# Convolution taps and gate tanh in two token halves, and a backward scan of one link per step, in a one-core hybrid encoder layer

## The chip, the cores and the metric

The kernel runs on one core of one Trainium2 chip, as one program. The metric is the device time of one execution in microseconds (us); of several runs the median counts. Five engines have queues of their own, each worked off in order: PE (TensorE, the matrix products), DVE (VectorE), ACT (ScalarE), POOL (GpSimd) and SP (SyncE, which here only issues transfers). PEld in the profile is the loading of weights into PE.

## The reference

One encoder layer for 1024 tokens of width 1024, all in float32. What the change touches is the state-space branch (SSD) and what goes ahead of it:

```python
def depthwise_conv_centred(u, w, bias):                 # 5 taps, padding 2 on both sides, per channel
    ...
    return out + bias.astype(u.dtype)

def ssd_branch(z, xbc, dt_raw, ...):
    xbc = jax.nn.silu(depthwise_conv_centred(xbc, conv_w, conv_b))
    xs, Bm, Cm = ...                                    # 32 heads of 64, 8 groups of B and C (state 128)
    dt = jax.nn.softplus(dt_raw + dt_bias)              # one for each direction
    y_fwd = ssd_chunked(xs, dt[:, :, 0], A[0], Bm, Cm)
    y_bwd = fl(ssd_chunked(fl(xs), fl(dt[:, :, 1]), A[1], fl(Bm), fl(Cm)))
    y = (y_fwd + y_bwd + d_skip * xs) * silu(z)
    ...                                                 # RMSNorm in 8 groups
```

`ssd_chunked` works in chunks of 128 tokens: within a chunk a masked product of C, B and the decays, and between chunks a scan `carry = carry * decay + state`, forward in one direction and backward in the other. The rest of the layer (windowed attention with a sink, gates `sigmoid(gate) * branch`, output projection, cross-attention into a normalised memory of 256 tokens, a squared-ReLU MLP, the final norm) is not touched.

## The kernel before

A matrix product in float32 is made of three passes with split operands (`mm3`, lines 85, 89 and 90): 8 such triples for 512 tokens by 128 channels, so 48 matmuls for all 1024 tokens. `phase0` normalises memory and input, writes the memory's keys and values, and computes the time steps (`dt_part`). `ssd_phase` then works through 8 groups of four heads. For each group it runs jobs on PE, in an order written out by hand: four convolution jobs (two tiles of x, one of B, one of C, numbers 0 to 3), one gate job, and one job for z. A convolution job computes a tile of 128 channels by 1024 tokens (`fm_chunks`, tokens 0 to 511 first: its "first half") into a PSUM tile `cps` of two banks; `conv_post` then makes ACT write weight 2 times the tile plus the bias into `acc`, DVE add the four other taps one after the other, ACT take a tanh and DVE multiply (SiLU). Such PSUM tiles have two buffers.

Between the triples of a job, at the counts in the table `at`, work on the scan of the group before is issued: `step(q, c)` for chunk c from 7 down to 0. On PE a step is `cb` of the next chunk (C times B), four small products with the decays `ef`, and `yo` (C times the carried states `prev`); on DVE it is the mask product of `ef` and `cb`, `t`, and three steps on `y`; on POOL two steps on `p1` and two affine selects on the decay rows, which ACT turns into `ef` and `eb` with eight exponentials. All jobs of a group but z's have a step, or the transposes of x (`tm_x`, in job 3), behind triple 8, that is between their halves, and most have another behind triple 16.

PE's order is that of the code (manual schedule). The order on the other engines is chosen by a scheduler when the program is built, and each engine then works through its own list. The backward chain of a group, six links of two POOL instructions each, is issued in `back` at the end of the z job. In `phase0` the row of norm weights for x is spread over 128 partitions by two matmuls (line 228) that stand behind the transposes of the normalised memory.

Of the kernel before, what the change touches and what calls it, by code (L numbers as in the profile page):

```python
# [7 lines left out]
F32 = mybir.dt.float32  # L8
F32R = mybir.dt.float32r
I32 = mybir.dt.int32  # L10
AF = mybir.ActivationFunctionType
ALU = mybir.AluOpType
# [4 lines left out]
P = 128  # L17
S = 1024
D = 1024
NT = 8  # L20
# [4 lines left out]
NEG = -1.0e30  # L25
# [139 lines left out]
def phase0(kx, ins, dr):  # L165
    nc, tc = kx.nc, kx.tc
    V, A, PE = nc.vector, nc.scalar, nc.tensor
    with tc.tile_pool(name="p0", bufs=1, side="right") as p0, tc.manual_schedule(engines={mybir.EngineType.PE}):
# [52 lines left out]
        wk.append(weight(ins["wxk"][1]))  # L221
        xs.append(load(ins["x"][P:2 * P]))
        gb = [psum_g(kx, "gb") for _ in range(2)]
        for h in range(2):
            PE.matmul(gb[0][:, h * 512:(h + 1) * 512], ones, gr[:, 0, h * 512:(h + 1) * 512], start=True, stop=True)
        for j in range(2):
            mem_split(rows(xm[j], gb[0]), j * P)
            PE.matmul(gb[1][:, j * 512:(j + 1) * 512], ones, gr[:, 1, j * 512:(j + 1) * 512], start=True, stop=True)
        kx.hT = [act_tiles(kx) for _ in range(2)]
        wv = []  # L230
        for t in range(NT):
# [15 lines left out]
def dt_part(kx, ins, dr, p0):  # L247
# [79 lines left out]
    for src, dst in ((keep, kx.coef), (acc, kx.ebias), (e, kx.ecs)):  # L327
# [3 lines left out]
            if j == 0:  # L331
                kx.tc.keep_in_program_order(t)
        A.activation(dst, pt.rearrange("p (j d s h) -> p s j d h", j=4, d=2, s=2), AF.Copy)
    conv_post(kx, kx.first, 2, cps)


def gate_block(kx, ins, dr, m, pool=None, pin=False):
# [22 lines left out]
def fm_chunks(kx, ps, w, halves=(0, 1)):  # L360
    ws = wsplit(w)
    for h in halves:
        for k in range(NK):
            mm3(kx, ps[:, h * 512:(h + 1) * 512], ws[k], act_pair(kx.hT[h], k), k == 0, k == NK - 1)
            yield
# [6 lines left out]
def conv_post(kx, q, i, ps):  # L372
    V, A = kx.nc.vector, kx.nc.scalar
    ca = kx.conv_pool
    tag = ("cx", "cx", "cB", "cC")[i]
    j = 4 * q.g + i
    cw = lambda k: kx.cw[:, 5 * j + k:5 * j + k + 1]
    acc = ca.tile([P, S], F32, tag=tag, bufs=2 if i < 2 else 1, name=tag)
    A.activation(acc, ps, AF.Identity, bias=kx.cb[:, j:j + 1], scale=cw(2))
    for k in (1, 3, 0, 4):  # L380
        o = k - 2
        if o < 0:
            V.scalar_tensor_tensor(acc[:, -o:], ps[:, :S + o], cw(k), acc[:, -o:], ALU.mult, ALU.add)
        else:
            V.scalar_tensor_tensor(acc[:, :S - o], ps[:, o:], cw(k), acc[:, :S - o], ALU.mult, ALU.add)  # L385
    th = ca.tile([P, S], F32, tag="tab", bufs=2, name="th")
    A.activation(th, acc, AF.Tanh)
    V.scalar_tensor_tensor(acc, th, 1.0, acc, ALU.add, ALU.mult)
    if i < 2:
        q.cx.append(acc)  # L390
    else:
        setattr(q, ("BT", "CT")[i - 2], acc)


def first_tiles(kx, ins, dr):

    q = kx.first = Group(0)
    ws = [wload(kx, ins["wssd"][0, i]) for i in range(2)]
    pss = [psum_g(kx, "cps") for _ in range(2)]
    for h in range(2):  # L400
        for i in range(2):
            for _ in fm_chunks(kx, pss[i], ws[i], (h,)):
                pass
    w = wload(kx, ins["wg"][0])
    gps = [kx.pp.tile([P, 512], F32, tag="p", name="gps") for _ in range(2)]
    for h in range(2):
        gemm_fm(kx, gps[h], w, kx.hT[h])
    for i in range(2):
        conv_post(kx, q, i, pss[i])
    gt = kx.conv_pool.tile([P, 2, 512], F32, tag="tab", bufs=2, name="gt")  # L410
    for h in range(2):
        kx.nc.scalar.activation(gt[:, h], gps[h], AF.Tanh, scale=0.5)
        kx.nc.sync.dma_start(dr.gt[0][h], gt[:, h])


def ssd_phase(kx, ins, dr):
# [4 lines left out]
    with tc.tile_pool(name="p1", bufs=1) as sp, tc.manual_schedule(engines={mybir.EngineType.PE}):  # L421
# [4 lines left out]
        def heads(ap):  # L426
            return ap.rearrange("p (h q) -> p h q", h=4)
# [3 lines left out]
        def conv_job(q, i):  # L431
            def load():
                return wload(kx, ins["wssd"][q.g, i])

            def run(w):
                ps = psum_g(kx, "cps")
                yield from fm_chunks(kx, ps, w)
                conv_post(kx, q, i, ps)
            return load, run

        def gate_job(m):
            def load():
                return wload(kx, ins["wg"][m])

            def run(w):
                ps = psum_g(kx, "gps")
                yield from fm_chunks(kx, ps, w)
                gt = ca.tile([P, 2, 512], F32, tag="tab", bufs=2, name="gt")
                for h in range(2):
                    A.activation(gt[:, h], ps[:, h * 512:(h + 1) * 512], AF.Tanh, scale=0.5)  # L450
                    nc.sync.dma_start(dr.gt[m][h], gt[:, h])
            return load, run
# [42 lines left out]
        def decay(q, d, c):  # L495
            o = 64 * d + 32 * (c // 4) + 4 * q.g
            return kx.dec[:, o:o + 4, c % 4:c % 4 + 1].broadcast_to([P, 4, 64])
# [15 lines left out]
            if c > 0:  # L513
                A.activation(prev[:, c - 1, 1], st[:, 256:], AF.Copy)

        def back(q):
            prev = q.prev
            for c in range(NT - 2, 0, -1):
                t = sp.tile([P, 256], F32, tag="p1", bufs=2, name="cb_t")
                G.tensor_tensor(heads(t), heads(prev[:, c, 1]), decay(q, 1, c), ALU.mult)  # L520
                G.tensor_tensor(prev[:, c - 1, 1], prev[:, c - 1, 1], t, ALU.add)  # L521

        def prep(q, c):
            b, j = c // 4, c % 4
            rows = sp.tile([P, 2, 4, P], F32, tag="rows", bufs=2, name="rows")
            for d in range(2):
                o = 64 * d + 32 * b + 4 * q.g
                nc.scalar.dma_start(rows[:, d], dr.cs[o:o + 4, j * P:(j + 1) * P].partition_broadcast(P))
            G.affine_select(out=rows[:, 0], in_=rows[:, 0], compare_op=ALU.is_ge, fill=NEG, base=0,  # L529
                            pattern=[[0, 4], [1, P]], channel_multiplier=-1)  # L530
            G.affine_select(out=rows[:, 1], in_=rows[:, 1], compare_op=ALU.is_ge, fill=NEG, base=0,  # L531
                            pattern=[[0, 4], [-1, P]], channel_multiplier=1)
            ef = q.efs[c] = sp.tile([P, 4, P], F32, tag="ef", bufs=3, name="ef")
            eb = sp.tile([P, 4, P], F32, tag="eb", bufs=2, name="eb")
            with tc.issue_after(q.zt[8 - c].ins) if c > 4 else ExitStack():
                for h in range(4):
                    o = 4 * q.g + h
                    A.activation(ef[:, h], rows[:, 0, h], AF.Exp, bias=kx.ebias[:, b, j, 0, o:o + 1])  # L538
                    A.activation(eb[:, h], rows[:, 1, h], AF.Exp, bias=kx.ebias[:, b, j, 1, o:o + 1])  # L539
            V.tensor_tensor(ef, ef, eb, ALU.add)  # L540
# [8 lines left out]
        def step(q, c):  # L549
# [23 lines left out]
            G.tensor_tensor(heads(p1), heads(q.xtok[:, c]), dsk[:, q.hs].unsqueeze(2).broadcast_to([P, 4, 64]), ALU.mult)  # L573
            if d1 - d0 == 2:
                G.tensor_tensor(p1, p1, t[:, 1], ALU.add)
            y = q.yz[j] = sp.tile([P, 256], F32, tag="yz", bufs=8, name="yz")
            V.tensor_tensor(y, cb[:, 256:], t[:, d0], ALU.add)
            V.tensor_tensor(y, y, p1, ALU.add)
# [23 lines left out]
        for g in range(NG):  # L602
# [10 lines left out]
            at = {8 * c + 8: [(state, q, c)] for c in range(NT)}  # L613
            at[4] = [(tm_b, q)]
            at[56] += [(prep, q, 7)]
            at[64] += [(prep, q, 6), (back, q), (mask, q, 7)]
            job(z_job(q), at)
        q = gs[7]
        job(gate_job(8), {6: [(step, q, 7)], 12: [(step, q, 6)]})
# [1092 lines left out]
```

## Time and profile before

| What | us |
|---|---|
| Median of 3 runs (2375.48 to 2376.95) | 2375.82 |
| Profiled execution, its own time | 2374.8 |
| Its span, first to last instruction | 2373.0 |
| PE busy | 2328.3 |
| DVE busy | 1567.7 |
| ACT busy | 1124.2 |
| POOL busy | 865.4 |

The profiled execution lies 1.0 us under the median and 1.8 us over its own span. A row of the timeline reads: start, duration, engine, line, operation, output from inputs, shape, count, and in brackets how long the engine had been idle and what ended that. A wait is put down to the instruction that came last before it ended.

### The profile page before, as it was taken

Reading aid. Unit: us, or ns where it says so; the run is one execution under the profiler, and the core shown is the slowest. Engines: PE = TensorE matmul, PEld = TensorE weight load, DVE = VectorE, ACT = ScalarE, POOL = GpSimd, SP = SyncE. Lnnn points to the kernel's source line nnn. Section 1 sums busy time; section 2 is a strip of 40 time slices with the busy share of each in tenths; the row PEclk is TensorE's granted clock in tenths of the full one; section 3 lists DMA queues with packets and bytes.
Section 4 is the critical chain, followed back from the end, with each engine's and each line's share of the span. In section 5 each row is a group of like instructions: output and inputs, shape, how many; then the busy total and the mean of one; then the engine's idle time right before and its main releaser. Section 6 shows DMA issues by size and latency. Waiting matters only on the chain.

```text
span 2373.0 us, 32192 instructions
## 1 busy us (share of the span) xinstructions
PE 2328.3 (98%) x11812; PEld 1930.2 (81%) x11812; DVE 1567.7 (66%) x2523; ACT 1124.2 (47%) x2398; POOL 865.4 (36%) x827
## 2 busy tenths in 40 slices
PE   9999999999999999999999999999999999999998
PEld 7888888888888887877777888888987887788887
DVE  4757566565756654375658987975685456689984
ACT  4445545555554555387765543345543333234341
POOL 2244536263443625255541013305475444200010
PEclk9999999999999999999999999999999999999999
DMA  6223323232322323111116247203253345722301
GB/s 219 84 77 98 87 83 115 72 107 68 111 78 92 107 75 104 45 36 54 39 52 228 101 151 266 89 1 98 98 173 125 110 135 175 281 94 77 128 27 71
DMA packets 150033, 251.01 MB, mean 106 GB/s; under 512 B 11250, under 2 KB 86130, under 8 KB 149876
## 3 DMA queue, kind: packets, MB, share of 16 engines
q1 hardware_dynamic: 79264, 210.67, 26.3%
q10 hardware_dynamic: 70612, 38.29, 5.7%
q8 instruction: 93, 1.52, 0.3%
q14 instruction: 64, 0.52, 0.1%
HBM read 201.47 MB, written 47.45 MB: 105 GB/s over the span
## 4 chain that ended last, share of the span: by engine, by line
PE 70%; DVE 12%; POOL 7%; ACT 5%; issue 4%; DMA 2%; POOLq 0%; ACTq 0%; SPq 0%; DVEq 0%
PE dps L1482 10%; PE mps L1482 8%; PE pb L1277 5%; PE pc L1277 3%; PE zp L89 3%; PE zp L85 2%; PE zp L90 2%; PE cps L90 2%; PE cps L85 2%; PE cps L89 2%; PE st L506 2%; POOL prev L521 2%; DVE cx L385 1%; PE mps L85 1%; POOL cb_t L520 1%
## 5 line engine op out<-in xcount | busy, mean ns | idle before, releaser
L69 POOL TENSOR_TENSOR wlo<-raw,whi 128x1024 fp32r<-128x1024 f32 x104 | 255.0, 2453 | 471.9 <-ACT whi L66 459.1
L1433 ACT ACTIVATE kt<-row 128x512 fp32r<-128x512 f32 x264 | 144.0, 620 | 185.8 <-PE dps L1482 83.2
L1482 PE MATMUL mps<-kt 128*128 128x512 f32 x1008 | 230.5, 390 | 1.5 <-DVE kt L1434 1.5
L1482 PE MATMUL dps<-kt 128*128 128x512 f32 x1008 | 228.6, 389 | 0.0
L1482 PEld LDWEIGHTS mps<-kt 128*128 128x128 f32 x1008 | 188.7, 188 | 42.1 <-DVE kt L1434 3.1
L1482 PEld LDWEIGHTS dps<-kt 128*128 128x128 f32 x1008 | 189.2, 188 | 39.3
L85 PE MATMUL cps<-kt,whi 128*128 128x512 f32 x512 | 215.0, 420 | 0.0
L66 ACT ACTIVATE whi<-raw 128x1024 fp32r<-128x1024 f32 x104 | 109.6, 1055 | 203.5 <-DMA raw<-in_wa_dram 42.7
L90 PE MATMUL cps<-kt,wlo 128*128 128x512 f32 x512 | 200.0, 391 | 0.0
L89 PE MATMUL cps<-kt,whi 128*128 128x512 f32 x512 | 199.4, 389 | 0.0
L1434 DVE TENSOR_TENSOR kt<-row,kt 128x512 fp32r<-128x512 f32 x264 | 171.9, 698 | 4.1 <-ACT kt L1433 4.0
L124 POOL TENSOR_TENSOR rr<-rv,mhalf 128x1 f32<-128x1 f32 (+1 forms) x50 | 35.0, 701 | 239.4 <-DVE rv L122 237.6
L529 POOL TENSOR_SCALAR_AFFINE_SELECT rows<-rows 128x512 f32<-128x512 f32 x64 | 44.2, 691 | 202.5 <-DMA rows<-d_cs 201.6
L1223 POOL TENSOR_TENSOR wop<-w,wop 128x512 fp32r<-128x512 f32 x64 | 86.0, 1347 | 85.8 <-ACT wop L1222 79.9
L89 PEld LDWEIGHTS cps<-kt,whi 128*128 128x128 f32 x512 | 96.3, 188 | 25.4 <-issue 6.7
L85 PEld LDWEIGHTS cps<-kt,whi 128*128 128x128 f32 x512 | 96.2, 188 | 25.1 <-issue 6.7
L90 PEld LDWEIGHTS cps<-kt,wlo 128*128 128x128 f32 x512 | 96.1, 188 | 20.7
L85 PE MATMUL gps<-kt,whi 128*128 128x512 f32 x240 | 102.2, 426 | 0.0
L539 ACT ACTIVATE eb<-rows,ebias 128x128 f32<-128x128 f32 x256 | 89.1, 392 | 23.3 <-POOL rows L531 23.3
L719 DVE CUSTOM_DVE_ANT_0 t<-sps,bias 128x384 f32<-128x384 f32 (+1 forms) x128 | 64.4, 522 | 51.6 <-PE sps L718 49.6
L730 POOL TENSOR_SCALAR t<-t,den 128x384 f32<-128x384 f32 (+1 forms) x128 | 69.2, 560 | 80.3 <-DVE den L728 70.8
L538 ACT ACTIVATE ef<-rows,ebias 128x128 f32<-128x128 f32 x256 | 90.1, 391 | 14.7 <-PE cb L561 14.7
(372 smaller groups left out, 6387.6 us busy)
## 6 DMA issues: line engine op xcount, KB each, us to landing
rows<-d_cs ACTq DMA_DIRECT2D x128, 256.0 KB, 3.8
raw<-in_wssd_dram SPq DMA_DIRECT2D x48, 512.0 KB, 3.6
raw<-in_wup_dram SPq DMA_DIRECT2D x40, 512.0 KB, 3.8
d_u<-c SPq DMA_DIRECT2D x64, 256.0 KB, 2.6
row<-in_wdn_dram SPq DMA_DIRECT2D x28, 512.0 KB, 6.6
row<-d_u SPq DMA_DIRECT2D x28, 512.0 KB, 6.6
x<-in_x_dram SPq DMA_DIRECT2D x16, 512.0 KB, 6.2
raw<-in_wg_dram SPq DMA_DIRECT2D x16, 512.0 KB, 3.5
```

Of the source, the lines that this page charges most:

```text
L66: steps = [nc.scalar.activation(hi, raw, AF.Copy)]
L69: steps.append((eng or nc.gpsimd).tensor_tensor(lo, raw, hi.bitcast(F32), ALU.subtract))
L85: i = mm(out, l[0], r[0], start=first, stop=False)
L89: mm(out, l[0], r[1], start=False, stop=False)
L90: mm(out, l[1], r[0], start=False, stop=last)
L538: A.activation(ef[:, h], rows[:, 0, h], AF.Exp, bias=kx.ebias[:, b, j, 0, o:o + 1])
L539: A.activation(eb[:, h], rows[:, 1, h], AF.Exp, bias=kx.ebias[:, b, j, 1, o:o + 1])
L1223: self.kx.nc.gpsimd.tensor_tensor(t[:, 1], src, t[:, 0].bitcast(F32), ALU.subtract)
L1277: self.kx.nc.tensor.matmul(ps, w[:, i, ks], act[:, k, j], start=start and k == 0 and m == 0, stop=k == 3 and m == 2, skip_group_check=True)
L1433: nc.scalar.activation(t[:, j, 0], src, AF.Copy)
L1434: nc.vector.tensor_tensor(t[:, j, 1], src, t[:, j, 0].bitcast(F32), ALU.subtract)
L1482: self.kx.nc.tensor.matmul(ps[t], lt[:, k, x, ts], rt[:, k, y], start=n in (1, 2, 5) and k == 0 and m == 0, stop=k == 3 and m == 2, skip_g ...
```

## The change

`conv_post` becomes a generator that does tokens 0 to 509 and then 510 to 1023, each with its weight-2 term, four taps, tanh and product. A convolution job starts the first part after its first half of matmuls, and after whatever the table places behind triple 8; the second part follows its second half. The gate jobs take the tanh and the store of each half behind that half. In `dt_part` and `first_tiles` both parts still follow the whole tile. `back` makes one link and is called in each `step` for chunks 7 to 2, behind the latest affine select. The two matmuls of norm weights for x move ahead of the transposes.

```diff
-        for h in range(2):
-            PE.matmul(gb[0][:, h * 512:(h + 1) * 512], ones, gr[:, 0, h * 512:(h + 1) * 512], start=True, stop=True)
+        for i in range(2):
+            for h in range(2):
+                PE.matmul(gb[i][:, h * 512:(h + 1) * 512], ones, gr[:, i, h * 512:(h + 1) * 512], start=True, stop=True)
         for j in range(2):
             mem_split(rows(xm[j], gb[0]), j * P)
-            PE.matmul(gb[1][:, j * 512:(j + 1) * 512], ones, gr[:, 1, j * 512:(j + 1) * 512], start=True, stop=True)
...
-    A.activation(acc, ps, AF.Identity, bias=kx.cb[:, j:j + 1], scale=cw(2))
-    for k in (1, 3, 0, 4):
-        o = k - 2
-        if o < 0:
-            V.scalar_tensor_tensor(acc[:, -o:], ps[:, :S + o], cw(k), acc[:, -o:], ALU.mult, ALU.add)
-        else:
-            V.scalar_tensor_tensor(acc[:, :S - o], ps[:, o:], cw(k), acc[:, :S - o], ALU.mult, ALU.add)
-    th = ca.tile([P, S], F32, tag="tab", bufs=2, name="th")
-    A.activation(th, acc, AF.Tanh)
-    V.scalar_tensor_tensor(acc, th, 1.0, acc, ALU.add, ALU.mult)
...
+    th = ca.tile([P, S], F32, tag="tab", bufs=2, name="th")
+    for a, b in ((0, 510), (510, S)):
+        A.activation(acc[:, a:b], ps[:, a:b], AF.Identity, bias=kx.cb[:, j:j + 1], scale=cw(2))
+        for k in (1, 3, 0, 4):
+            o = k - 2
+            l, r = max(a, -o), min(b, S - o)
+            V.scalar_tensor_tensor(acc[:, l:r], ps[:, l + o:r + o], cw(k), acc[:, l:r], ALU.mult, ALU.add)
+        A.activation(th[:, a:b], acc[:, a:b], AF.Tanh)
+        V.scalar_tensor_tensor(acc[:, a:b], th[:, a:b], 1.0, acc[:, a:b], ALU.add, ALU.mult)
+        yield
...
             def run(w):
                 ps = psum_g(kx, "cps")
-                yield from fm_chunks(kx, ps, w)
-                conv_post(kx, q, i, ps)
+                post = None
+                for h in range(2):
+                    yield from fm_chunks(kx, ps, w, (h,))
+                    post = post or conv_post(kx, q, i, ps)
+                    next(post)
...
                 ps = psum_g(kx, "gps")
-                yield from fm_chunks(kx, ps, w)
                 gt = ca.tile([P, 2, 512], F32, tag="tab", bufs=2, name="gt")
                 for h in range(2):
+                    yield from fm_chunks(kx, ps, w, (h,))
                     A.activation(gt[:, h], ps[:, h * 512:(h + 1) * 512], AF.Tanh, scale=0.5)
...
-        def back(q):
+        def back(q, c):
             prev = q.prev
-            for c in range(NT - 2, 0, -1):
-                t = sp.tile([P, 256], F32, tag="p1", bufs=2, name="cb_t")
-                G.tensor_tensor(heads(t), heads(prev[:, c, 1]), decay(q, 1, c), ALU.mult)
-                G.tensor_tensor(prev[:, c - 1, 1], prev[:, c - 1, 1], t, ALU.add)
+            t = sp.tile([P, 256], F32, tag="cbt", bufs=1, name="cb_t")
+            G.tensor_tensor(heads(t), heads(prev[:, c, 1]), decay(q, 1, c), ALU.mult)
+            G.tensor_tensor(prev[:, c - 1, 1], prev[:, c - 1, 1], t, ALU.add)
...
             if d1 - d0 == 2:
                 G.tensor_tensor(p1, p1, t[:, 1], ALU.add)
+            if c > 1:
+                with tc.issue_after(q.shut.ins):
+                    back(q, c - 1)
...
-            at[64] += [(prep, q, 6), (back, q), (mask, q, 7)]
+            at[64] += [(prep, q, 6), (mask, q, 7)]
```

On PE, in the convolution job 0 of group 2, around the step for chunk 7 that stands between the job's halves: the last matmul of the first half, the step, and the first matmul of the second half. `cps` is the job's PSUM tile, `kt` a tile of normalised input (`kt_254` holds the second 512 tokens), `whi` and `wlo` the two parts of the weights. The brackets name the engines whose counters the instruction waits for. Before:

```order
L90 MATMUL cps_2383<-kt_253,wlo_2040 128x512
L545 MATMUL cb_2408<-cC_2030,cB_1919 128x128 [waits Activation_49]
L561 MATMUL cb_2372<-xtok_1965,ef_2294 128x64 [waits DVE_49]
L561 MATMUL cb_2372<-xtok_1965,ef_2294 128x64 x3
L565 MATMUL yo_2436<-prev_2072,cC_2030 128x256 [waits Activation_49]
L85 MATMUL cps_2383<-kt_254,whi_2039 128x512
```

The same place in the changed kernel:

```order
L90 MATMUL cps_2421<-kt_253,wlo_2096 128x512
L549 MATMUL cb_2446<-cC_2039,cB_1898 128x128 [waits Activation_49]
L565 MATMUL cb_2410<-xtok_2014,ef_2350 128x64 [waits DVE_49]
L565 MATMUL cb_2410<-xtok_2014,ef_2350 128x64 x3
L569 MATMUL yo_2474<-prev_2128,cC_2039 128x256 [waits Activation_49]
L85 MATMUL cps_2421<-kt_254,whi_2095 128x512 [waits DVE_49,Activation_49]
```

No matmul moved, but the first matmul of the second half has a wait for DVE and one for ACT that it did not have. In the built program the counts that it waits for are those of the last of the four first-half taps of the same tile, and of ACT's weight-2 term that begins them. All 29 convolution jobs of `ssd_phase` have it; the 10 gate jobs have one for ACT, on the tanh of the first half.

On DVE at the same step: `t` and `yz` belong to the step, `cx` is the convolution's result. Before, with the whole-tile taps a step later:

```order
L547 TENSOR_TENSOR ef_2343<-ef_2343,cb_2408 128x512 [waits PE_49]
L569 TENSOR_TENSOR t_2438<-yo_2436,ecs_178 128x256 [waits PE_49]
L577 TENSOR_TENSOR yz_2442<-cb_2372,t_2438 128x256 [waits DVE_49]
L540 TENSOR_TENSOR ef_2483<-ef_2483,eb_2484 128x512 [waits Activation_49]
L578 TENSOR_TENSOR yz_2442<-yz_2442,p1_2440 128x256 [waits DVE_49,Pool_49]
L579 TENSOR_TENSOR yz_2442<-yz_2442,zs_2045 128x256 [waits DVE_49]
L547 TENSOR_TENSOR ef_2420<-ef_2420,cb_2471 128x512 [waits PE_49]
L383 SCALAR_TENSOR_TENSOR cx_2510<-cps_2383,cols_380,cx_2510 128x1023 [waits Activation_49]
```

In the changed kernel:

```order
L551 TENSOR_TENSOR ef_2399<-ef_2399,cb_2446 128x512 [waits PE_49]
L573 TENSOR_TENSOR t_2476<-yo_2474,ecs_178 128x256 [waits PE_49]
L390 SCALAR_TENSOR_TENSOR cx_2488<-cps_2421,cols_380,cx_2488 128x509 [waits Activation_49]
L584 TENSOR_TENSOR yz_2483<-cb_2410,t_2476 128x256 [waits DVE_49]
L390 SCALAR_TENSOR_TENSOR cx_2488<-cps_2421,cols_380,cx_2488 128x510 [waits DVE_49]
L585 TENSOR_TENSOR yz_2483<-yz_2483,p1_2478 128x256 [waits DVE_49,Pool_49]
L390 SCALAR_TENSOR_TENSOR cx_2488<-cps_2421,cols_380,cx_2488 128x508 [waits DVE_49]
L586 TENSOR_TENSOR yz_2483<-yz_2483,zs_2101 128x256 [waits DVE_49]
L390 SCALAR_TENSOR_TENSOR cx_2488<-cps_2421,cols_380,cx_2488 128x510 [waits DVE_49]
```

The four half taps now stand between the step's own instructions, and behind `t`, which waits for the step's `yo` on PE.

On ACT, in the convolution job 3 of the same group 2, around the copies of the transposed x (`xtok` from `tm`): `cC` is the job's own result, `cB` that of the job before, `yz` and `rr` belong to the norm of the finished scan, `yts` to the store of the transposed y. Before:

```order
L584 ACTIVATE yz_2735<-yz_2735,rr_2915 128x256
L483 ACTIVATE xtok_2967<-tm_2968 128x4x128 [waits PE_49]
L483 ACTIVATE xtok_2967<-tm_2974 128x4x128 [waits PE_49]
L387 ACTIVATE th_2927<-cB_2921 128x1024 [waits DVE_49]
L483 ACTIVATE xtok_2967<-tm_2980 128x4x128 [waits PE_49]
L483 ACTIVATE xtok_2967<-tm_2986 128x4x128 [waits PE_49]
L66 ACTIVATE whi_3379<-raw_3381 128x1024 [waits DMAHW7_49,PE_49]
L594 ACTIVATE yts_3021<-yt_3016,cols_380 128x512 [waits DMAHW0_49,PE_49]
L594 ACTIVATE yts_3029<-yt_3024,cols_380 128x512 [waits DMAHW1_49,PE_49]
L379 ACTIVATE cC_3032<-cps_2942,cols_380 128x1024
```

In the changed kernel:

```order
L591 ACTIVATE yz_2987<-yz_2987,rr_2994 128x256 [waits Activation_49,Pool_49]
L591 ACTIVATE yz_2923<-yz_2923,rr_2994 128x256
L591 ACTIVATE yz_2871<-yz_2871,rr_2994 128x256
L591 ACTIVATE yz_2803<-yz_2803,rr_2994 128x256
L391 ACTIVATE th_2929<-cB_2928 128x514 [waits DVE_49]
L488 ACTIVATE xtok_3044<-tm_3045 128x4x128 [waits PE_49]
L488 ACTIVATE xtok_3044<-tm_3051 128x4x128 [waits PE_49]
L488 ACTIVATE xtok_3044<-tm_3057 128x4x128 [waits PE_49]
L488 ACTIVATE xtok_3044<-tm_3063 128x4x128 [waits PE_49]
L386 ACTIVATE cC_3069<-cps_3019,cols_380 128x510
```

The weight-2 term of the job's first half, from which its taps start, now stands right behind four scalings, a tanh and four copies; before, the whole-tile term stood behind the copies of the transposed y, after the whole tile was done on PE, and no PE instruction of the same job waited for it.

More of the change, by code (lines that the diff above doesn't have):

```diff
@@ L333, in dt_part @@
         A.activation(dst, pt.rearrange("p (j d s h) -> p s j d h", j=4, d=2, s=2), AF.Copy)
-    conv_post(kx, kx.first, 2, cps)
+    for _ in conv_post(kx, kx.first, 2, cps):
+        pass
 def gate_block(kx, ins, dr, m, pool=None, pin=False):
@@ L408, in first_tiles @@
     for i in range(2):
-        conv_post(kx, q, i, pss[i])
+        for _ in conv_post(kx, q, i, pss[i]):
+            pass
     gt = kx.conv_pool.tile([P, 2, 512], F32, tag="tab", bufs=2, name="gt")
@@ L530, in prep @@
                             pattern=[[0, 4], [1, P]], channel_multiplier=-1)
-            G.affine_select(out=rows[:, 1], in_=rows[:, 1], compare_op=ALU.is_ge, fill=NEG, base=0,
-                            pattern=[[0, 4], [-1, P]], channel_multiplier=1)
+            q.shut = G.affine_select(out=rows[:, 1], in_=rows[:, 1], compare_op=ALU.is_ge, fill=NEG, base=0,
+                                     pattern=[[0, 4], [-1, P]], channel_multiplier=1)
             ef = q.efs[c] = sp.tile([P, 4, P], F32, tag="ef", bufs=3, name="ef")
```

## The prediction

> **What bounds the kernel now.** I read the page's sums first, then the stretch of the state-space branch in the table by stage, then PE's waits, then PE, DVE and ACT in order of time around one conv job of each kind.
>
> ```profile
> span 2373.0 us, 32192 instructions
> ...
> PE 2328.3 (98%) x11812; PEld 1930.2 (81%) x11812; DVE 1567.7 (66%) x2523; ACT 1124.2 (47%) x2398; POOL 865.4 (36%) x827
> ```
>
> ```profile
> 100.00:900.00 800.00, 790.57 (x4490) 669.00 (x4488) 490.43 (x713) 403.00 (x960) 367.66 (x387) 1.00 0.31 92
> ```
>
> ```profile
> PE yo L565 <- DVE t L569: 6.7, 10, 1.0
> PE pb L1277 <- DVE c L1346: 3.0, 2, 1.8
> ```
>
> PE bounds it: 2328.3 of 2373.0 us busy, so all gains together can't pass 44.7 us. Between 100 and 900 us (columns: length, then PE, weight loads, DVE, ACT and POOL, the granted clock, the DMA share, GB/s), where all but the first convolutions lie, PE is busy 790.57 of 800 at a granted clock of 1.00, DVE (490.43) 61%, ACT (403.00) 50%. The largest wait of PE there is for `t`: 6.7 us in ten pieces. So the change can win little, and it loses whatever it makes PE wait. The order shown above says that it does: the first matmul of each second half waits for the last first-half tap of the same tile. The sum is therefore 29 walks from the end of a first half (call it H) to that tap.
>
> **Head (gain 2.0).**
>
> ```profile
> 8.51 1.97 PE L191 MATMUL nt<-ident,xn 128*128 128x128 f32 x8 [1.98 <-DVE xn L143]
> 10.41 2.07 PE L228 MATMUL gb<-gr,ones 1*128 1x512 f32 x2
> ```
>
> The norm weights for x take two pairs of 2.07. Ahead of the transposes the first pair fills the idle 1.98, and the second costs there what it saves behind: `kxp` starts 2.0 sooner. Ends: 0 (if `xn` is what sets the second transposes) and 2.07; I take 2.0, since the second transposes waited for nothing.
>
> **The half taps.** Job 0 has a 256-wide step between its halves, job 2 a 512-wide one. On PE, with `cb` the first and `yo` the last product of the step, and `cps` the second half:
>
> ```profile
> 261.39 0.38 PE L545 MATMUL cb<-cC,cB 128*128 128x128 f32 x2
> ...
> 262.45 0.65 PE L565 MATMUL yo<-prev,cC 128*128 128x256 f32 x2
> 262.75 0.58 PE L85 MATMUL cps<-kt,whi 128*128 128x512 f32 x1
> ```
>
> ```profile
> 268.41 0.38 PE L545 MATMUL cb<-cC,cB 128*128 128x128 f32 x2
> ...
> 269.47 1.08 PE L565 MATMUL yo<-prev,cC 128*128 128x512 f32 x2
> 269.98 0.79 PE L85 MATMUL cps<-kt,whi 128*128 128x512 f32 x1
> ```
>
> Prices on DVE, start to start. A whole tap is 1.19, and a 512-wide operation half of it, so a half tap is 0.60 and two halves cost what one whole did:
>
> ```profile
> 276.96 1.28 DVE L385 SCALAR_TENSOR_TENSOR cx<-cps,cols,cx 128x1023 f32<-128x1023 f32 x1
> 278.15 0.42 DVE L577 TENSOR_TENSOR yz<-cb,t 128x256 f32<-128x256 f32 x1
> ```
>
> ```profile
> 284.75 0.68 DVE L569 TENSOR_TENSOR t<-yo,ecs 128x512 f32<-128x512 f32 x1
> 285.36 0.68 DVE L540 TENSOR_TENSOR ef<-ef,eb 128x512 f32<-128x512 f32 x1
> ```
>
> A 256-wide one is 0.34 (287.12 to 287.46). A tap right behind the tap that it needs costs 0.13 more (322.01 to 323.33 is 1.32):
>
> ```profile
> 287.12 0.42 DVE L579 TENSOR_TENSOR yz<-yz,zs 128x256 f32<-128x256 f32 x1
> 287.46 0.68 DVE L547 TENSOR_TENSOR ef<-ef,cb 128x512 f32<-128x512 f32 x1
> ```
>
> ```profile
> 322.01 1.28 DVE L383 SCALAR_TENSOR_TENSOR cB<-cps,cols,cB 128x1022 f32<-128x1022 f32 x1
> 323.33 1.28 DVE L385 SCALAR_TENSOR_TENSOR cB<-cps,cols,cB 128x1022 f32<-128x1022 f32 x1
> ```
>
> `t` starts 0.04 after its `yo` ends (262.45+0.65 is 263.10), and a PE that waited resumes 0.15 after DVE ends (284.75+0.68 is 285.43):
>
> ```profile
> 263.14 0.42 DVE L569 TENSOR_TENSOR t<-yo,ecs 128x256 f32<-128x256 f32 x1 [0.64 <-PE yo L565]
> ```
>
> ```profile
> 285.58 1.09 PE L565 MATMUL yo<-prev,cC 128*128 128x512 f32 x2 [0.76 <-DVE t L569]
> ```
>
> - Job 0: `yo` ends at H+1.71 (263.10−261.39). Then 0.04, `t` 0.34, and by the new order tap, y, tap, y, tap, y, tap: 3×(0.60+0.34), the last tap with its whole duration, 0.68, and 0.15. That is H+5.74. PE could have gone on at H+1.36 (262.75−261.39): **4.4**.
> - Job 2: tap 1 lies ahead of `t`; `yo` ends at H+2.14 (270.55−268.41). Then 0.04, `t` 0.60, tap and y twice (2×0.94), 0.68 and 0.15: H+5.49, against H+1.57 (269.98): **3.9**.
> - Job 1 has the same kind of step as job 2, but its last taps stand behind the y steps that want POOL's `p1`, and `p1` can stand behind a split of weights:
>
> ```profile
> L69 POOL TENSOR_TENSOR wlo<-raw,whi 128x1024 fp32r<-128x1024 f32 x53 | 128.4, 2422 | 171.6 <-ACT whi L66 163.9 <-PE dtps L273 7.7
> ```
>
> Ends 3.9, and 6.3 with one split of 2.42 in front; no row says which, so about the middle: **5.2**.
>
> Job 3 has the transposes of x there instead of a step, and ACT is what its taps wait for. PE, then ACT, then the price of a 512-wide ACT operation from PSUM:
>
> ```profile
> 323.18 1.91 PE L482 MATMUL tm<-ident,cx 128*128 128x128 f32 x16
> ```
>
> ```profile
> 323.19 1.71 ACT L584 ACTIVATE yz<-yz,rr 128x256 f32<-128x256 f32 x4 [1.86 <-POOL rr L124]
> 324.80 1.06 ACT L483 ACTIVATE xtok<-tm 128x512 f32<-128x512 f32 x2
> ```
>
> ```profile
> L473 ACT ACTIVATE zs<-zp 128x512 f32<-128x512 f32 x32 | 19.0, 595 | 52.4 <-PE zp L90 52.4
> ```
>
> - Job 3: from 324.80 a tanh and four copies at 0.48 each (pairs take 1.06, the second one's tail with it), then the weight-2 term 0.60: 327.8. Four taps in a row, 3×0.73 + 0.68, and 0.15: 330.8. PE would be free at 325.1 (323.18+1.91): 5.7. The norm ahead of the scalings stands behind half taps instead of whole ones and comes slightly sooner: **5.6**.
> - Group 0's job 3 has no norm in front, but by the order its taps stand among seven other operations of DVE. At 5.6 and four of those at 0.60 it is **8**; ends 5.6 and 9.8.
> - Gate jobs: PE waits only for ACT's tanh of the half, 0.6. Behind a step (1.36 or more, above) that is hidden. Gate jobs 8 and 10 have no step behind triple 8: 0.6 and what stands ahead of it on ACT, **1.0** each. Without the cover the eight others could lose 1 each as well.
>
> Sum: 4.4+5.2+3.9+5.6 is 19.1; by 7 groups 133.7; with 8 and 2.0, 143.7.
>
> **What else moves.** The ten waits of `yo` (6.7) come from `t` behind whole taps. With half taps, and PE held up longer elsewhere, they vanish: −6.7. In each of 32 tiles DVE issues five instructions more, ACT two. The work is the same (two halves cost one whole), on engines with 39% and 50% free; where it is late, the walks have priced it.
>
> ```profile
> L521 POOL TENSOR_TENSOR prev<-prev,cb_t 128x256 f32<-128x256 f32 x48 | 41.7, 869 | 3.1
> L520 POOL TENSOR_TENSOR cb_t<-prev,dec 128x256 f32<-128x256 f32 x48 | 29.8, 621 | 3.1
> ```
>
> The 48 links, 1.49 each (869+621 ns), go from one burst of six per group into the steps, one ahead of each next `yo`. Steps stand some 7 us apart (261.39, 268.41), and POOL has 54% free (367.66 of 800 busy), so I cost the links at nothing. That free time is the cover; without it a link delays its `yo` by up to 1.49.
>
> Net: 143.7 − 2.0 − 6.7 = +135.0. On the profiled execution's 2374.8 that is 2509.8; the median lies 1.0 above that execution: **2511**.
>
> **Rivals.**
>
> *The clock restarts.* Before, no wait that this change meets is over 1.8 us, and the granted clock is 1.00. The new gaps are 3.9 to 8. At the head, after idle time, sixteen `kxp` took 5.81 where later ones took 3.62:
>
> ```profile
> 16.31 5.81 PE L203 MATMUL kxp<-mT,w 128*128 128x256 f32 x16
> ...
> 22.82 3.62 PE L203 MATMUL kxp<-mT,w 128*128 128x256 f32 x16
> ```
>
> The table by stage for PE alone has the granted clock in the third column from the right:
>
> ```profile
> 8.00:16.00 8.00, 7.49 (x20) 1.00 1.01 400
> 16.00:24.00 8.00, 8.00 (x31) 1.00 0.38 127
> ```
>
> The slow sixteen cost 2.19 more, my price of a restart. If the eight gaps of job 3 cost it, +17.5: 2528. If all over 4.3 do (22), +48.2: 2559. Against it: PE had been busy for 7.49 of the 8 us before those slow `kxp`, so the row may show something else than idle time.
> The Trainium skill, page "TensorE: Matmul & The Clock Gate", section "Part 1: The HAM clock gate (the "warmup" mystery)", says that the clock falls to half after an idle window of about 3.4 us, and that these windows run freely. By it a gap of 3.9 would seldom hold a whole window and one of 5.6 mostly, so the time would lie at 2528 rather than 2559. The slow `kxp` fits; the granted clock, 1.00 in both rows, doesn't show it; and this trace has no such gap to judge by.
>
> *No stall (the other side).* The wait costs nothing where the last tap ends before PE arrives, at H+1.36 to H+1.57. Against it, `yo` alone ends at H+1.71 and `t` follows; for it, the first tap does stand ahead of `t` in job 2, and it decides if all four came to stand there and ended within those 1.4 us. If every wait were met, only the gains would be left: 2374.8−8.7+1.0 = 2367.
> The Trainium skill, page "PSUM — Partial Sum Buffer", section "PSUM bank collisions raise a hardware error", says that engines on different banks run clean, and the first-half taps read the first bank alone. By this the chip would let PE go on, and the sum would be 2367; but the wait stands in the program, whatever the chip allows, and no row of before shows the case.
>
> *Links late.* Splits of 2.42 run on POOL between the steps, and a link behind one could hold up its `yo`: 48 by some 1.0 us, +48, 2559. Against it: each step now has 4 us more.
>
> *Stalls half as large*, if the taps mostly fit in ahead of `t`: 71.8 instead of 143.7, 2439.
>
> **How the numbers follow.** Stalls without restarts 0.50, with its own range of 2480 to 2540: job 1 at its ends moves it by 9, the eight gate jobs by 8, group 0 by 2, and a tenth on all walks by 14. Stalls with restarts 0.36 (2528 to 2559); links late 0.05; half stalls 0.04; no stall 0.05. The range leaves out no stall and half stalls, and ends a little beyond the restarts: 2470 to 2565. About 0.2% (4.8 us) is what a measurement tells from no change. Faster has the no-stall case, 0.05; ends that happen to cancel 0.02; slower 0.93.
>
> **What would show it.** In PE's waits, L85 `cps` behind DVE's tap 21 to 29 times, 110 to 145 us in all, the longest 5 to 8, and next to none on `t`. PE's busy time within 5 us of 2328; if it is 15 to 60 more, and matmuls behind the gaps last longer, the clock restarted. The first `kxp` starts near 14.3. On POOL one pair of L520 and L521 to a step. I am wrong if that wait of L85 is under 1 us in the mean, or if POOL or ACT ends it in jobs 0 and 2.

## The result, and the profile after

The changed kernel takes 2600.48 us (median of 5 runs, 2599.40 to 2603.32) against 2375.48 for the kernel before: a ratio of 1.095, 95% interval 1.0935 to 1.0965. The direction was right, the size was not: 225 us were lost where 135 were forecast, and the time lies 35 us above the top of the range.

The page of the changed kernel, its stretch of convolutions in the table by stage, and PE's waits there (total, times, longest):

```profile
span 2601.5 us, 32391 instructions
...
PE 2400.4 (92%) x11812; PEld 1978.1 (76%) x11812; DVE 1589.3 (61%) x2683; ACT 1142.2 (44%) x2462; POOL 877.7 (34%) x827
```

```profile
100.00:1100.00 1000.00, 831.77 (x4322) 689.91 (x4320) 496.93 (x844) 406.72 (x983) 360.65 (x366) 0.90 0.23 71
```

```profile
PE cps L85 <- DVE cx L390: 92.9, 14, 9.2
PE cps L85 <- DVE cC L390: 49.6, 8, 9.6
PE cps L85 <- DVE cB L390: 24.9, 7, 3.8
```

Two losses are to be seen. The span is 228.5 us longer. PE's idle time rose from 44.7 to 201.1 (+156.4): the 29 new waits of a second half's first matmul for a half tap make 167.4 us, and other waits shrank by some 11. And PE's busy time rose by 72.1 with the same 11812 matmuls; between 100 and 1100 us the mean granted clock (third number from the right) is 0.90, where it was 1.00 before. One group's four gaps on PE, in jobs 0, 1, 2 and 3:

```profile
309.81 0.77 PE L85 MATMUL cps<-kt,whi 128*128 128x512 f32 x1 [5.04 <-DVE cx L390]
...
335.97 0.76 PE L85 MATMUL cps<-kt,whi 128*128 128x512 f32 x1 [8.62 <-DVE cx L390]
...
370.85 0.77 PE L85 MATMUL cps<-kt,whi 128*128 128x512 f32 x1 [3.51 <-DVE cB L390]
...
394.35 0.77 PE L85 MATMUL cps<-kt,whi 128*128 128x512 f32 x1 [5.71 <-DVE cC L390]
```

And what follows such a gap, here that of job 3 in the group before:

```profile
258.64 0.76 PE L85 MATMUL cps<-kt,whi 128*128 128x512 f32 x1 [5.72 <-DVE cC L390]
259.20 0.63 PE L89 MATMUL cps<-kt,whi 128*128 128x512 f32 x1
259.62 0.63 PE L90 MATMUL cps<-kt,wlo 128*128 128x512 f32 x1
...
263.85 0.39 PE L85 MATMUL cps<-kt,whi 128*128 128x512 f32 x1
264.08 0.39 PE L89 MATMUL cps<-kt,whi 128*128 128x512 f32 x1
```

From start to start the matmuls take 0.42 us at first (259.20 to 259.62) and 0.23 from 263.85 on. Summed over the matmuls behind a gap, the excess over 0.227, the step at full speed, is 1.4 to 2.95 us, 69.3 us for the 29.

### The profile page after: what moved, and what is told of

It reads as the page before. It is cut to its first block, busy times and chain, and to the rows that moved or that the text cites. A ratio compares the mean times of both kernels' runs of the same rounds, so it can differ in the third digit from the quotient of the medians.

```text
span 2601.5 us, 32391 instructions
## 1 busy us (share of the span) xinstructions
PE 2400.4 (92%) x11812; PEld 1978.1 (76%) x11812; DVE 1589.3 (61%) x2683; ACT 1142.2 (44%) x2462; POOL 877.7 (34%) x827
## 4 chain that ended last, share of the span: by engine, by line
PE 66%; DVE 15%; ACT 6%; DMA 5%; issue 4%; POOL 3%; ACTq 0%; SPq 0%; POOLq 0%; DVEq 0%
PE dps L1489 9%; PE mps L1489 7%; PE pb L1284 5%; PE cps L85 4%; PE cps L89 4%; PE cps L90 3%; PE pc L1284 3%; PE zp L89 2%; PE zp L90 2%; PE zp L85 2%; PE st L511 2%; DMA rows<-d_cs 2%; DMA raw<-in_wssd_dram 2%; DVE cx L390 1%; POOL wlo L69 1%
## 5 line engine op out<-in xcount | busy, mean ns | idle before, releaser
L85 PE MATMUL cps<-kt,whi 128*128 128x512 f32 x512 | 239.2, 467 | 168.8 <-DVE cx L390 92.9
L85 PEld LDWEIGHTS cps<-kt,whi 128*128 128x128 f32 x512 | 113.0, 221 | 212.4 <-issue 150.8
L89 PE MATMUL cps<-kt,whi 128*128 128x512 f32 x512 | 225.3, 440 | 0.0
L90 PE MATMUL cps<-kt,wlo 128*128 128x512 f32 x512 | 223.3, 436 | 0.0
L89 PEld LDWEIGHTS cps<-kt,whi 128*128 128x128 f32 x512 | 113.2, 221 | 27.4 <-issue 3.4
L90 PEld LDWEIGHTS cps<-kt,wlo 128*128 128x128 f32 x512 | 111.9, 218 | 27.2
L551 DVE TENSOR_TENSOR ef<-ef,cb 128x512 f32<-128x512 f32 x64 | 43.9, 685 | 140.8 <-PE cb L549 140.4
L390 DVE SCALAR_TENSOR_TENSOR cx<-cps,cols,cx 128x510 f32<-128x510 f32 (+5 forms) x128 | 94.4, 742 | 8.8 <-ACT cx L386 8.7
L1284 PE MATMUL pb<-kt,wop 128*128 128x512 f32 x384 | 94.6, 396 | 2.4 <-ACT c L1338 2.4
```

The lines of the kernel that those rows point to most:

```text
L85: i = mm(out, l[0], r[0], start=first, stop=False)
L89: mm(out, l[0], r[1], start=False, stop=False)
L90: mm(out, l[1], r[0], start=False, stop=last)
L390: V.scalar_tensor_tensor(acc[:, l:r], ps[:, l + o:r + o], cw(k), acc[:, l:r], ALU.mult, ALU.add)
L1284: self.kx.nc.tensor.matmul(ps, w[:, i, ks], act[:, k, j], start=start and k == 0 and m == 0, stop=k == 3 and m == 2, skip_group_check=True)
```

## The experiments

Two theories stood against each other. W: the wait for the whole PSUM tile, and slow matmuls behind each gap, make all of the loss. L: the links on POOL, the gate halves, or the number and order of the instructions make a good part of it. Each run is compared with runs of the kernel before on the same chip (medians 2377.7 to 2378.6 there).

**Parts of the change alone.** The convolution's halves put into the kernel before, nothing else:

```diff
-                yield from fm_chunks(kx, ps, w)
-                conv_post(kx, q, i, ps)
+                post = None
+                for h in range(2):
+                    yield from fm_chunks(kx, ps, w, (h,))
+                    post = post or conv_post(kx, q, i, ps)
+                    next(post)
```

> The kernel before with only the convolution's halves; links in one burst, gates whole, norm weights where they were. Theory W: the whole loss is here, 2595 to 2620 us, with about 169 us of gaps at the second halves and 70 us of slow matmuls behind them. Rival L: a good part of the loss needs the links or the gate halves, under 2560.

Measured: 2636.99 us, ratio 1.1085 (1.1069 to 1.1101), 17 us above W's range. The conv halves alone carry the loss, and more of it than the whole change. The spans of the two profiles differ by 33 us, and some 24 of them are job 0: its gaps are 8.1 us here against 4.25 to 5.09 there. DVE, then POOL, around one of them:

```profile
316.07 0.93 DVE L583 TENSOR_TENSOR yz<-yz,p 128x256 f32<-128x256 f32 x1 [2.91 <-POOL p L578]
316.92 0.73 DVE L390 SCALAR_TENSOR_TENSOR cx<-cps,cols,cx 128x508 f32<-128x508 f32 x1
```

```profile
314.84 0.62 POOL L525 TENSOR_TENSOR cb_t<-prev,dec 128x256 f32<-128x256 f32 x1
315.42 0.61 POOL L578 TENSOR_TENSOR p<-xtok,dsk 128x256 f32<-128x256 f32 x1
```

The burst of backward links holds `p1` back to 315.42, DVE's step on `y` waits 2.91 us for it, and the last two taps stand behind that step. So, by these rows, the links per step, costed at nothing, repair 3.4 us in each of seven gaps.

The links alone:

```diff
-            at[64] += [(prep, q, 6), (back, q), (mask, q, 7)]
+            at[64] += [(prep, q, 6), (mask, q, 7)]
...
+            if c > 1:
+                with tc.issue_after(q.shut.ins):
+                    back(q, c - 1)
```

> The kernel before with only the backward link per step. The forecast had the links cost nothing and counted the ten yo waits (6.7 us) for the half taps. In the run with head and links PE waits for nothing between 110 and 960 us, where before it was idle 10 of 850 us. Theory B (the burst of links on POOL was what made t and the next steps late): those 10 us are won by the links alone, 2362 to 2369 us where before is 2376. Rival (links are neutral, as forecast): 2374 to 2378.

Measured: 2362.61 us, ratio 0.9937 (0.9923 to 0.9950). In the stretch from 110 to 870 us (second number: PE busy) the kernel before has the first row, this one the second; below them DVE's step on `y` with `p1`, before and now:

```profile
110.00:870.00 760.00, 752.20 (x4268) 636.40 (x4267) 471.17 (x682) 386.47 (x916) 349.94 (x364) 1.00 0.30 91
```

```profile
110.00:870.00 760.00, 760.00 (x4346) 645.00 (x4345) 480.66 (x693) 392.92 (x931) 358.51 (x368) 1.00 0.31 93
```

```profile
L578 DVE TENSOR_TENSOR yz<-yz,p 128x256 f32<-128x256 f32 x56 | 31.6, 564 | 56.5 <-POOL p L575 32.4 <-POOL p L573 23.9
```

```profile
L580 DVE TENSOR_TENSOR yz<-yz,p 128x256 f32<-128x256 f32 x56 | 27.5, 491 | 32.9 <-POOL p L574 32.6
```

PE has no gap left there. The 23.9 us that DVE waited for the first instruction of `p1` (L573 before) are gone, and with them the ten waits of `yo`: they came from the burst on POOL, not from the whole taps ahead of `t`, as I had put it.

The norm weights alone (the first hunk of the diff):

> The kernel before with only the norm weights moved ahead of the transposes. The forecast: 2.0 us. In the run with head and links the time steps began 5.1 us sooner than before, of which 0.6 was an earlier first transfer and 2.1 the first sixteen kxp (3.72 instead of 5.81 us); in the changed kernel these sixteen stayed at 5.58. So 2370.5 to 2374 us where before is 2376.

Measured: 2373.82 us, ratio 0.9982 (0.9972 to 0.9992). A gain of some 4 us; the interval is 1.9 to 6.7, so that it doesn't tell 4 from the forecast 2.0. The first `kxp` starts at 13.48, and the first sixteen take 3.72 instead of 5.81:

```profile
13.48 3.72 PE L203 MATMUL kxp<-mT,w 128*128 128x256 f32 x16 [0.91 <-ACT mT L192]
```

The gate halves alone:

```diff
-                yield from fm_chunks(kx, ps, w)
                 gt = ca.tile([P, 2, 512], F32, tag="tab", bufs=2, name="gt")
                 for h in range(2):
+                    yield from fm_chunks(kx, ps, w, (h,))
                     A.activation(gt[:, h], ps[:, h * 512:(h + 1) * 512], AF.Tanh, scale=0.5)
```

> The kernel before with only the gate jobs' tanh and store per half. The forecast: 2.0 us for gate jobs 8 and 10, nothing for the eight others, at most 1 each. The whole-tap run waited 19.2 us in ten gate jobs. Theory W: a whole-tile wait as in the conv jobs, on an ACT that is late behind the conv job before, whatever the links: PE waits 15 to 25 us at the gates, some of these gaps are followed by slow matmuls, 2388 to 2402 us. As forecast: 2376 to 2386.

Measured: 2424.17 us, ratio 1.0193 (1.0179 to 1.0207), more than W expected. Eight gaps of 3.6 to 6.0 us and one of 0.7, and slow matmuls behind the eight. PE's wait, and ACT's rows ahead of the first gap's end:

```profile
PE gps L85 <- ACT gt L450: 34.4, 9, 6.0
```

```profile
191.46 1.04 ACT L387 ACTIVATE th<-cx 128x1024 f32<-128x1024 f32 x1
193.71 0.42 ACT L580 ACTIVATE zs<-yz 128x256 f32<-128x256 f32 x1 [1.21 <-DVE yz L579]
...
194.12 0.58 ACT L450 ACTIVATE gt<-gps 128x512 f32<-128x512 f32 x1
```

The gate's tanh stands behind the tanh of the conv job before, which starts only when the last of four whole taps ends on DVE (191.30), and behind an operation on the finished `y` (`zs`) that waits another 1.21 us for DVE's `yz`, which stands behind the same taps.

**Whole taps, late parts, two tiles.** Three runs take the wait of the conv jobs away in different manners and keep the rest of the change. First, the taps on the whole tile again (`conv_post` and its calls as before):

> The changed kernel with the convolution's taps, tanh and product on the whole tile again, behind both halves; the moved norm weights, the backward link per step and the gate halves stay. Theory W (PE's wait for the whole PSUM tile in the middle of a conv job, and slow matmuls after each of these gaps, make all of the loss): no cps row among PE's waits, PE busy back at 2328, 2366 to 2375 us, that is 0 to 9 below before. Rival L (late links on POOL, or the other moved work, make a good part of it): 2420 or more.

Measured: 2383.05 us, ratio 1.0017 (1.0007 to 1.0028). The conv waits are gone, and all but some 5 us of the loss with them; yet the time lies 8 us above the expected range, since the gates now wait:

```profile
PE gps L85 <- ACT gt L450: 19.2, 10, 2.9
```

Second, both parts of the halves behind the second half's matmuls:

```diff
-                post = None
-                for h in range(2):
-                    yield from fm_chunks(kx, ps, w, (h,))
-                    post = post or conv_post(kx, q, i, ps)
-                    next(post)
+                yield from fm_chunks(kx, ps, w)
+                for _ in conv_post(kx, q, i, ps):
+                    pass
```

> The changed kernel with the same two parts of conv_post, but both issued behind the second half of the matmuls, so that DVE and ACT do the same 160 and 64 extra instructions and no matmul of the job stands behind them. Theory W: 2366 to 2378 us, no cps row among PE's waits. Rival N (the number of instructions or their order on DVE and ACT makes the loss, the wait only shows it): over 2420.

Measured: 2413.06 us, ratio 1.0150 (1.0133 to 1.0168), between the two ranges. The conv waits are gone here too, so the 160 and 64 extra instructions are not what cost 225 us. What is left is again the gates, later still (3.98 to 5.74 us in seven of them, with slow matmuls behind each). So rival N has a small part: against the whole taps these instructions cost 30 us, by way of the gates.

```profile
PE gps L85 <- ACT gt L453: 37.2, 10, 5.7
```

Third, the halves in the middle of the job as in the change, but each half in a PSUM tile of one bank; two columns at the seam are added apart:

```diff
-                ps = psum_g(kx, "cps")
+                ps = [kx.ph.tile([P, 512], F32, tag="h", name="cps") for _ in range(2)]
...
+            if h and o < 0:
+                V.scalar_tensor_tensor(acc[:, 512:512 - o], ps[0][:, 512 + o:], cw(k), acc[:, 512:512 - o], ALU.mult, ALU.add)
```

> The changed kernel with the two halves of each conv and gate job in PSUM tiles of one bank each, so that a first-half tap and a second-half matmul no longer share a tile; the columns at the seam are added by two small operations of DVE per tile. The first half is still post-processed in the middle of the job. Theory W: no stall and no slow matmuls, 2362 to 2374 us. If the chip itself can't write one bank while DVE reads its neighbour, or if the taps in the middle of the job delay the step's t: over 2400.

Measured: 2388.79 us, ratio 1.0049 (1.0035 to 1.0062). No second half waits for the first-half taps of its own job any more, while DVE taps one bank and PE writes the other, at full speed (0.23 us from start to start). So the wait was the program's, on the tile, and not the chip's. The time is 15 us above the expected range; the trace shows other waits, of the transposes for ACT's stores of `y`, and one of 4.9 in group 0's job 3. That one ends with L391, the taps on the B tile that `dt_part` still makes as a whole:

```profile
PE tm L520 <- ACT yts L634: 14.4, 7, 2.5
PE cps L85 <- DVE cB L391: 4.9, 1, 4.9
```

**The slow matmuls.** Products that nobody reads fill the gaps. `fill` writes them into the next job's tile:

```diff
                     next(post)
+                    if h == 0:
+                        fill((9, 17, 6, 11 if q.g else 19)[i])
```

> The changed kernel with products that nobody reads put on PE ahead of each second half of a conv job (9, 17, 6 and 11 of 512 columns in jobs 0 to 3, 19 in group 0), written into the next job's PSUM tile: PE is busy through most of each gap, but the gap stays. If idle time is what slows the matmuls behind a gap, they run at 0.23 us from start to start again and the time falls by 50 to 72 from 2600, to 2530 to 2550 us, with 160 us of fill on PE. If they are slow for another reason (traffic of DVE and ACT, weights, the PSUM tile), the time stays at 2590 to 2610.

Measured: 2647.21 us, ratio 1.1131 (1.1116 to 1.1146). My price was wrong: a product took 0.86 us, not 0.46, so that the 320 of them took 275 us and overran the gaps. So this time tells nothing, though the mean granted clock was 0.997 again. So once more with about half of them:

> As the run with fill, but with 5, 9, 3, 6 products (9 in group 0): the fill took 0.86 us for each product instead of the 0.46 reckoned with, and so overran the gaps. At 0.86 these are 4.3, 7.7, 2.6, 5.2 and 7.7 us, inside gaps of 4.7, 8.6, 3.5, 5.7 and 9.6. If idle time slows the matmuls: the gaps stay as long as in the changed kernel, but the matmuls behind them run at 0.23 us, and the time is 2600 less 60 to 72, so 2528 to 2545 us. If not: 2590 to 2610.

Measured: 2537.58 us, ratio 1.0674 (1.0657 to 1.0690), 63 less than the changed kernel. PE still waits for the taps, now at most 1.4 us at a time behind the fill, and no matmul behind those rests is slow (in group 0's job 3 the fill itself waits 5.8 us, and there the clock falls):

```profile
PE cps L85 <- DVE cB L390: 7.1, 7, 1.4
PE cps L85 <- DVE cx L390: 6.1, 9, 1.1
```

With the gaps as long as before but PE busy in them, 63 us are back. Idle time of PE is what slows the matmuls.

How long must it be idle? Two taps fewer in the middle of the job make the gaps shorter:

```diff
+            if k == 0 and a == 0:
+                yield
             V.scalar_tensor_tensor(acc[:, l:r], ps[:, l + o:r + o], cw(k), acc[:, l:r], ALU.mult, ALU.add)
```

> The changed kernel with only the weight-2 term and two of the four taps of the first half in the middle of the job; the other two, tanh and product follow the second half. Theory W: the gaps shorten by about 1.3 to 1.9 us, to some 2.8, 6.7, 1.6 and 4.2 in jobs 0 to 3. In the whole-tap run the gaps of 1.92, 2.42, 2.88 and 2.92 were followed by slow matmuls and those of 1.70, 2.06 and 2.77 were not, and all of 3.5 and more were. If a gap of more than half of some 3.4 us that falls into one window is what counts, all of jobs 1 and 3 are slow, job 0 mostly and job 2 hardly ever; if a whole idle window of 3.4 us has to pass, only job 1 always is. Time 2490 to 2540.

Measured: 2520.87 us, in a single run. The gaps were 1.5 to 1.8 in job 2, 2.25 in job 0, 4.2 in job 3, 7 to 8 in job 1. All of jobs 1 and 3 were followed by slow matmuls, none of job 2, and of the seven equal gaps of job 0 four.

**Job 1.** Its gaps, 8.2 to 9.2 us, were the ones that I had far too low. In the changed kernel ACT and DVE do this ahead of the end of the gap at 335.97:

```profile
327.31 1.06 ACT L66 ACTIVATE z<-raw 128x1024 fp32r<-128x1024 f32 x1 [6.67 <-DMA raw<-in_wssd_dram]
328.27 0.61 ACT L391 ACTIVATE th<-cx 128x514 f32<-128x514 f32 x1
...
329.49 0.76 ACT L386 ACTIVATE cx<-cps,cols 128x510 f32<-128x510 f32 x1
```

```profile
328.92 2.42 DVE L392 SCALAR_TENSOR_TENSOR cx<-th,cx 128x514 f32<-128x514 f32 x1 [4.49 <-ACT th L391]
331.26 0.68 DVE L551 TENSOR_TENSOR ef<-ef,cb 128x512 f32<-128x512 f32 x1
331.86 0.74 DVE L390 SCALAR_TENSOR_TENSOR cx<-cps,cols,cx 128x509 f32<-128x509 f32 x1
```

ACT waits 6.67 us for a transfer of z's weights, with the tanh of job 0's second half and then job 1's weight-2 term behind it in the queue; DVE waits 4.49 for that tanh. Held back on ACT:

```diff
+                with tc.issue_after(kx.last_th.ins):
+                    return [wload(kx, ins["wssd"][q.g, 4], hi=zhl[0], lo=zhl[1]), wload(kx, ins["wssd"][q.g, 5])]
```

> The changed kernel with ACT's split of z's weights held behind the last tanh of job 2. In the changed kernel this split waits 6.7 us for its transfer at the head of ACT's queue in job 1, and the tanh and the weight-2 term of job 1's first half stand behind it. Theory: job 1's gap falls from 8.6 to about that of job 0 or 2, 3.5 to 5, in seven groups: 22 to 35 us less, 2565 to 2578; slow matmuls behind each gap stay. Rival (job 1's taps are late because of POOL's p1, as the forecast had it): the gap stays above 8 and the time at 2600.

Measured: 2583.08 us, ratio 1.0860 (1.0842 to 1.0878), 5 us above the expected range. Job 1's gaps fell to 5.3 to 6.9, some 2.8 each: z's split makes most of the 3.4 us by which the forecast for job 1 fell short, and the rival is out. What is left, 5.8 in the mean, was not taken apart; in the same group the weight-2 term now stands on ACT behind an exponential (`eb`) that waits 3.31 us for a select on POOL:

```profile
319.43 0.40 ACT L544 ACTIVATE eb<-rows,ebias 128x128 f32<-128x128 f32 x1 [3.31 <-POOL rows L536]
```

But job 3's gaps rose from 5.7 to 7.84, where z's split now stands on POOL ahead of the norm that ACT's scalings wait for; three quarters of the gain in gaps went there:

```profile
374.37 2.41 POOL L69 TENSOR_TENSOR z<-raw,z 128x1024 fp32r<-128x1024 f32 x1 [15.36 <-ACT z L66]
376.88 1.02 POOL L124 TENSOR_TENSOR rr<-rv,mhalf 128x4 f32<-128x4 f32 x1
```

**What beats both.** The moved norm weights and the links, with convolution and gate on whole tiles:

> The kernel before with only the moved norm weights and the backward link per step: convolution and gate on whole tiles. The whole-tap run was held up 19.2 us by PE waiting for ACT's tanh in the gate jobs, and lost some 8 more to slow matmuls behind four of these gaps. Theory W: with the gate whole again both are gone, no gps row among PE's waits, 2360 to 2374 us where before is 2375 to 2378. Rival L (the links cost something): 2378 or more, with yo waiting for POOL's prev.

Measured: 2358.99 us, ratio 0.9919 (0.9905 to 0.9934), just below the expected range and the lowest ratio of all; its interval overlaps that of the links alone. PE has no wait between 110 and 860 us:

```profile
110.00:860.00 750.00, 750.00 (x4284) 636.22 (x4283) 476.87 (x688) 385.07 (x916) 356.61 (x367) 1.00 0.30 92
```

## Why the prediction was wrong, point by point

- **The mechanism of the wait** was right: 29 waits, ended by DVE's taps. Without them (whole taps, or two tiles) all but 5 to 11 of the 225 us are gone.
- **The walks.** In the mean of seven: job 0 4.7 (forecast 4.4), job 2 3.6 (3.9), job 3 5.7 (5.6), group 0's job 3 9.6 (8), gates 1.7 (2.0). Job 1 was 8.6 (5.2), and this term was mis-sized: 24 of the 25 us by which the sum of the stalls fell short. I had looked for POOL's `p1` as its cause; 2.8 of the 3.4 us went when z's weight split no longer stood at the head of ACT's queue. It stands in the order of ACT, which I had only read in job 3.
- **The clock** is the step that failed most: the sum put the slow matmuls behind the gaps at nothing. I took "stalls without restarts" as the likeliest, and in the rival let only gaps over 4.3 us restart, 22 of them. All 29 did, at 2.4 each (my price was 2.19): 69 us. The forecast, with 25 for the stalls and 69 for the restarts, would have been 2605. What I held against it, that PE had been busy ahead of the slow `kxp`, was no reason. In the old trace these products start 0.43 us apart up to 20.31 us and 0.22 from 20.65 on, and its first record of the granted clock begins at 20.56 (the 1.00 that the table prints ahead of it stands for no record). They ran slow from the start of the program and not behind a gap (so did the transposes ahead of them, 1.97 us for eight where later ones took 1.04), so that my price of 2.19 came near 2.4 by luck. Behind the head the old trace has one gap of more than 1.8 us, 2.34 at `pb`, with full speed behind it: too little to speak against restarts.
- **The links** were costed at nothing, and the 6.7 us of `yo` were put down to whole taps. Alone the links win 0.6%. The burst on POOL ahead of `p1` stood in the trace (23.9 us of DVE's waits), and I had looked at it only as work to be moved.
- **The gate halves** came out as forecast, 1.7 us, but by luck: with PE held up in the conv jobs ACT is in time, which I had not seen. With that cover gone they cost 19 us of waits beside whole taps, and 1.9% alone. I had named this cover and priced its loss at 1 us a job.
- **The head** won about its 2.0 us in the changed kernel (`kxp` at 14.23 instead of 16.31), as forecast. Alone it won some 4. What these sixteen products take goes by when the clock comes up: of the ten traces with the moved weights, seven have their first record of the granted clock at 12.0 to 13.4 us and take some 3.7 us, and three, the changed kernel's among them, have it at 17.6 to 18.0 and take some 5.6.

```profile
14.23 5.58 PE L203 MATMUL kxp<-mT,w 128*128 128x256 f32 x16 [0.50 <-ACT mT L192]
```

## What to carry to other kernels

Splitting post-processing into halves brings nothing while the halves share a tile that the program guards as a whole: look in the order for a wait that the next matmul has gained, and give each half its own tile, which here took the wait away but won nothing over the kernel before (2388.79 us). A gap on PE has two prices, its length and the slow matmuls behind it, and a trace without gaps tells nothing of the second. Before costing a moved burst at nothing, read who waits for the instruction that stands behind it: here the part of the change that looked least was the one that won.

## What the runs showed of the hardware that I had not expected

The matmuls slow down behind far shorter gaps than I thought, and not by a fixed length of the gap. Over all traces above, by the length of PE's gap ahead of a conv or gate matmul:

| Gap | Followed by slow matmuls |
|---|---|
| up to 1.82 us | never |
| 1.92 to 2.92 | the 1.92, 2.42, 2.88 and 2.92 of the whole-tap run and four of seven of 2.25; not 2.06, 2.77 and three of 2.25 |
| 3.5 and more | always |

In the run with two taps, behind a gap of 2.25, the matmuls first run at full speed and slow down only 1.5 us after PE goes on, for 3.4 us (165.87 to 169.28):

```profile
164.41 0.47 PE L85 MATMUL cps<-kt,whi 128*128 128x512 f32 x1 [2.25 <-DVE cx L392]
164.72 0.40 PE L89 MATMUL cps<-kt,whi 128*128 128x512 f32 x1
...
165.87 0.63 PE L85 MATMUL cps<-kt,whi 128*128 128x512 f32 x1
166.29 0.63 PE L89 MATMUL cps<-kt,whi 128*128 128x512 f32 x1
...
169.28 0.39 PE L90 MATMUL cps<-kt,wlo 128*128 128x512 f32 x1
```

This would fit a gate that looks at stretches of some 3.4 us, running freely, and halves the clock when one was idle for more than about half: gaps over 3.4 then always fill half of one, and gaps from 1.7 to 3.4 do by chance. The traces bear it out, since they hold the stretches: in each of the 14 traces all records of the granted clock begin on one grid with a step of 3.41 us. In the whole-tap run the gap of 2.77 (183.06 to 185.83) falls into two of these stretches, and most of the gap of 2.88 (289.11 to 291.99) into one (columns: length, then PE, weight loads, DVE, ACT and POOL, the granted clock, the DMA share, GB/s):

```profile
180.63:184.04 3.41, 2.44 (x15) 1.53 (x13) 3.06 (x4) 2.58 (x6) 3.17 (x3) 1.00 0.86 281
184.04:187.46 3.42, 1.63 (x7) 1.36 (x8) 3.42 (x4) 2.07 (x6) 2.81 (x4) 1.00 0.52 164
187.46:190.87 3.41, 3.41 (x17) 2.83 (x16) 2.92 (x7) 1.72 (x5) 2.24 (x3) 1.00 0.58 177
```

```profile
289.86:293.27 3.41, 1.28 (x6) 1.06 (x7) 3.41 (x4) 2.41 (x6) 3.15 (x4) 1.00 0.52 157
293.27:296.69 3.42, 3.42 (x10) 2.65 (x9) 3.06 (x7) 1.38 (x4) 1.90 (x3) 0.50 0.58 183
```

PE is idle for 0.97 and 1.79 us of the first two, and the clock stays at 1.00; it is idle for 2.13 us of 289.86:293.27, and the next stretch has 0.50. Over all 14 traces no stretch at full clock with under 1.50 us of idle PE was followed by the half clock, and each with over 1.97 was; between the two both occur. The Trainium skill, page "TensorE: Matmul & The Clock Gate", section "Part 1: The HAM clock gate (the "warmup" mystery)", has such windows of about 3.4 us and the half clock. The slow spell of 3.4 us agrees; that a whole window must be idle does not: gaps of 3.51 were followed by slow matmuls each time, and four of 2.25 were.

DVE's product of two SBUF operands took 2.42 us (328.92, above) while POOL ran a weight split from 328.44 to 330.79; the same form in job 2 takes 0.69 in the mean.

```profile
328.44 2.35 POOL L69 TENSOR_TENSOR z<-raw,z 128x1024 fp32r<-128x1024 f32 x1 [0.16 <-ACT z L66]
```

```profile
L392 DVE SCALAR_TENSOR_TENSOR cB<-th,cB 128x514 f32<-128x514 f32 x8 | 5.5, 693 | 18.9 <-ACT th L391 18.9
```

In job 1 of groups 1 to 7 it took 2.42 to 2.76 each time beside this split, and 0.69 each time in the run that holds z's split back. The half taps, with one operand in PSUM, kept near 0.74. ACT's weight-2 term was done at 330.25 and the first tap began at 331.86, so I estimate that this adds up to 1.6 us to job 1's gap; it would then be part of the 2.8 that the run won there, and was not tried apart.
